# Attention: the softmax difference moved behind the next block's maxima, scores split from their maxima, two transposes later

## The chip, the cores and the metric

The kernel runs on one core of a Trainium2 chip. The metric is device time in microseconds (us) of one execution; lower is better. Five engines work from queues of their own, each strictly in the order in which its instructions stand: TensorE (PE in the rows; its weight loads are PEld), VectorE (DVE), ScalarE (ACT), GpSimd (POOL) and the queue that issues DMAs (SP).

## What is computed

One inference step of a small decoder: a convolution layer with a feed-forward layer, then a differential-attention layer with a feed-forward layer, for a prompt of 512 tokens and for 8 samples of 8 new tokens each with 512 cached positions. The change touches the attention of the prompt. Every head has two score matrices (c = 0, 1) and its weights are the difference of two softmaxes:

```python
def diff_weights(scores, q_pos, k_pos, rel_bias, lam):
    dist = q_pos[:, None] - k_pos[None, :]
    bias = jnp.transpose(rel_bias[rel_buckets(jnp.maximum(dist, 0))], (2, 0, 1)).astype(jnp.float32)
    logits = scores + bias[None, :, None]
    logits = jnp.where((dist >= 0)[None, None, None], logits, -jnp.inf)
    p = jax.nn.softmax(logits, axis=-1)
    return p[:, :, 0] - lam * p[:, :, 1]
```

`prompt_diff_attn` does this for 8 heads and 4 blocks of 128 queries; block i sees 128 (i + 1) keys. Its result times the values is normalised per head and goes through an output projection.

## The kernel before

All of it is one program for one core, written with tiles; a wrapper (line 62) keeps every engine's instructions in the order in which the Python code emits them, so nearly every row of the profile says L62 and is told apart by its tiles. The first part (convolution, feed-forward, projections to keys, queries and values) and the last part (output projection, second feed-forward) are not touched.

The attention stage is a plan of turns. `at(r, rank, f)` (line 1042) puts a function into turn r; `play` (line 1333) runs the functions of a turn by rank. Each function emits its instructions for all engines, so the ranks set the order on every engine at once. Head h takes four turns, and four more functions of older work are woven into each:

- **sample turn**, r = 4h: scores, maxima and exponent of sample h (`sample`, lines 1045 to 1154).
- **block-3 turn**, r = 4h + 1: the scores of query block 3 (512 keys), VectorE's maxima over them, ScalarE's exponentials (`prompt`, `scores`, line 1182). At its start stands `norm` of the sample (rank 0.2); behind the maxima stand the transposes of an older sample's output with ScalarE's copy of it to `xhi` (rank 2.2), and a 128x512 `xlo` of an older head (rank 2.5).
- **block-2 turn**, r = 4h + 2: the same for block 2 (384 keys); `low` of the sample, two small `xlo` (rank 0.5); `power` of the head before (rank 2.5): five VectorE operations, then GpSimd's `pow` of 128x4.
- **last-blocks turn**, r = 4h + 3: the same for blocks 1 and 0 (256 and 128 keys); values of an older sample (rank 2.47); `scale` of the head before (rank 2.3).

In `prompt` every block goes through four functions. `scores` issues six matmuls per block from `whi` and `wlo` into the two PSUM banks `bS[0]` and `bS[1]` (one for each c), and in the same function the maxima: a custom VectorE operation that adds the bias `Tb`, writes `pt` and leaves the row maximum in a small tile `sm`, followed by ScalarE's exponential. The next block's scores use the same two banks, so they wait for these maxima. `differ` (line 1205) is VectorE's: a reciprocal, a 128x1 product with lambda (`nlam`) and one pass over `pt`. `turn` (line 1218) transposes the result on TensorE (`c_rev,pt`) and copies it on ScalarE to `aT`. `values` multiplies by `vv`. Small tiles come from a pool of six buffers, `pt` from three, so a later tile can stand in the buffer of an earlier one and waits for its last reader.

```python
at(r, 2, scores)
at(r + 1, 0, differ)
at(r + 1, 5, turn)
at(r + 2, 5.1 if 3 in blocks else 3, values)
```

Of the kernel before, what the change touches and what calls it, by code (L numbers as in the profile page):

```python
# [36 lines left out]
def build(tc, A, O):  # L37
# [3 lines left out]
    with ctx:  # L41
# [38 lines left out]
        def sm(n=8):  # L80
            t = small.tile([128, 16], F32, name="sm")
            return t[:, :n]
# [529 lines left out]
        with tc.tile_pool(name="h0", bufs=1) as hp0:  # L612
# [29 lines left out]
            with tc.tile_pool(name="cv", bufs=1) as cvp:  # L642
                c = cvp.tile([128, KT, T], F32, name="c")
                smid = Stats()
                with tc.tile_pool(name="u", bufs=2) as up:
# [143 lines left out]
                    r = smid.tok_half(0)  # L789
# [18 lines left out]
                    for i, (k, hf) in enumerate(steps):  # L808
# [5 lines left out]
                        if i == 0:  # L814
                            r = smid.tok_half(1)
# [38 lines left out]
        with tc.tile_pool(name="kvq", bufs=1) as kp:  # L854
# [164 lines left out]
            with tc.tile_pool(name="att", bufs=2) as ap_:  # L1019
# [15 lines left out]
                def next_turn():  # L1035
                    turns[0] += 1
                    return bT[turns[0] % 2]
# [4 lines left out]
                def at(r, rank, f):  # L1042
                    plan.setdefault(r, []).append((rank, f))
# [134 lines left out]
                def prompt(X, blocks, r):  # L1178
                    st_ = {}
                    place = {i: (0 if x == 0 else 128 * (blocks[0] + 1)) for x, i in enumerate(blocks)}  # L1180

                    def scores():
                        pt_ = ap_.tile([128, 1024], F32, name="pt", bufs=3)
                        for i in blocks:
                            o, n = 2 * place[i], 256 * (i + 1)
                            st_[i] = (pt_[:, o:o + n].rearrange("p (c n) -> p c n", c=2), sm())
                        for i in blocks:
                            n, o = 128 * (i + 1), place[i]
                            for x, (a, b) in enumerate(((0, 0), (0, 1), (1, 0))):
                                for cc in range(2):  # L1190
                                    rows = slice(64 * cc, 64 * cc + 64)
                                    pe.matmul(bS[cc][:, o:o + n], lhsT=X.q2[a][rows, i * 128:(i + 1) * 128],
                                              rhs=X.k2[b][rows, :n], start=(x == 0), stop=(x == 2))
                        for i in blocks:
                            n, o = 128 * (i + 1), place[i]
                            t, m = st_[i]
                            for cc in range(2):
                                ve.tensor_tensor_reduce(out=t[:, cc, :], in0=bS[cc][:, o:o + n],
                                                        in1=X.Tb[:, 512 - n:512], scale=-1.0, scalar=3.0e38,
                                                        op0=ALU.add, op1=ALU.min, accum_out=m[:, cc:cc + 1])  # L1200
                                ac.activation(out=t[:, cc, :], in_=t[:, cc, :], func=AF.Exp, scale=-1.0,
                                              bias=m[:, cc:cc + 1],
                                              accum_out=(X.s0[:, i:i + 1] if cc == 0 else m[:, 2:3]))

                    def differ():
                        for i in blocks:
                            t, m = st_[i]
                            ve.reciprocal(out=m[:, 3:4], in_=m[:, 2:3])
                        for i in blocks:
                            t, m = st_[i]  # L1210
                            ve.tensor_scalar(out=m[:, 4:5], in0=X.s0[:, i:i + 1], scalar1=nlam, scalar2=m[:, 3:4],
                                             op0=ALU.mult, op1=ALU.mult)
                        for i in blocks:
                            t, m = st_[i]
                            ve.scalar_tensor_tensor(out=t[:, 0, :], in0=t[:, 1, :], scalar=m[:, 4:5],
                                                    in1=t[:, 0, :], op0=ALU.mult, op1=ALU.add)

                    def turn():
                        pT = next_turn()
                        o = 0  # L1220
                        for i in blocks:
                            for j in range(i + 1):
                                pe.transpose(out=pT[:, o + j * 128:o + (j + 1) * 128],
                                             in_=st_[i][0][:, 0, j * 128:(j + 1) * 128], identity=rev)
                            o += 128 * (i + 1)
                        aT = st_["aT"] = ap_.tile([128, 512], F32, name="aT", bufs=2)
                        ac.copy(out=aT[:, :o], in_=pT[:, :o])

                    def values():
                        o = 0  # L1230
                        for i in blocks:
                            for j in range(i + 1):
                                pe.matmul(X.po[:, i * 128:(i + 1) * 128],
                                          lhsT=st_["aT"][:, o + j * 128:o + (j + 1) * 128],
                                          rhs=vv[:, j, X.h * 128:(X.h + 1) * 128], start=(j == 0), stop=(j == i))
                            o += 128 * (i + 1)

                    at(r, 2, scores)
                    at(r + 1, 0, differ)
                    at(r + 1, 5, turn)  # L1240
                    at(r + 2, 5.1 if 3 in blocks else 3, values)

                def prompt_out(X, r):
# [52 lines left out]
                for h_ in range(H):  # L1296
                    X = Head()
                    X.last = h_ == H - 1
                    r = 4 * h_ + 1
                    sample(h_, r - 1)  # L1300
                    at(max(r - 3, 0), 6 if h_ else 0, lambda X=X, h_=h_: prepare(X, h_))
                    at(max(r - 1, 0), 0.1, lambda X=X: prepare_low(X))
                    prompt(X, (3,), r)
                    prompt(X, (2,), r + 1)
                    prompt(X, (1, 0), r + 2)
                    prompt_out(X, r + 4)
# [197 lines left out]
```

## Time and profile before

| | |
|---|---|
| median of 3 runs | 1350.44 us (1347.79 to 1351.11) |
| the profiled execution, its own time | 1349.65 us |
| its span | 1347.8 us |
| instructions | 25258 |
| TensorE matmul busy | 1329.7 us, 99% |
| TensorE weight loads busy | 1225.5 us, 91% |
| VectorE busy | 918.1 us, 68% |
| ScalarE busy | 599.1 us, 44% |
| GpSimd busy | 117.9 us, 9% |
| block-3 maxima of head 1 and of head 7, first row | at 803.21 and at 884.76 us of the span |

The profile shows one execution. Busy shares are averages over stages that have different limits, so the attention stage has to be read by itself. In the rows of the timeline the first number is the start in us from the beginning of the span, the second what the instruction (or the run of equal instructions) took; in square brackets stands the idle time of the engine before it, and what ended it. A matmul row covers several passes; its end is modelled.

### The profile page before, as it was taken

To read this page: it belongs to the slowest core of one execution; us is meant where nothing else is said; L and a number is where in the kernel's file an instruction comes from. 1 tells how busy PE (TensorE), PEld (TensorE's weight loads), DVE (VectorE), ACT (ScalarE), POOL (GpSimd) and SP (SyncE) were. 2 spreads that over 40 slices of the span, in tenths; PEclk is the share of its full clock that TensorE was granted. 3 is DMA by queue.
4 is the path that set the end of the run, shared out by engine and by line. 5 is a ranking of instruction groups with operands and counts; after the bars stand their busy time and mean duration, and the time that the engine had idled before them with its cause. 6 is when DMAs were issued, how large, how long until landed. Compare 5 with 4: busy or idle time off the path is not lost.

```text
span 1347.8 us, 25258 instructions
## 1 busy us (share of the span) xinstructions
PE 1329.7 (99%) x10320; PEld 1225.5 (91%) x10320; DVE 918.1 (68%) x1803; ACT 599.1 (44%) x1224; POOL 117.9 (9%) x112
## 2 busy tenths in 40 slices
PE   8999899999999999999999999999999999999998
PEld 7988399999999999998787766689999999999998
DVE  6999276798747757864555258876679855865862
ACT  5122273345524524544455347764434543543550
POOL 0001112000000000012222203232100000000000
PEclk9999999999999999999999999999999999999999
DMA  8765412131231231163214268964121331231121
GB/s 306 202 173 168 103 63 95 32 125 63 95 126 63 94 126 63 59 215 113 79 72 176 73 254 312 347 234 168 32 95 63 110 111 63 97 123 63 63 95 71
DMA packets 57398, 168.00 MB, mean 125 GB/s; under 512 B 5970, under 2 KB 12754, under 8 KB 57154
## 3 DMA queue, kind: packets, MB, share of 16 engines
q1 hardware_dynamic: 55552, 163.85, 34.8%
q10 hardware_dynamic: 1730, 2.54, 0.6%
q8 instruction: 81, 1.33, 0.4%
q14 instruction: 35, 0.29, 0.1%
HBM read 145.56 MB, written 10.56 MB: 116 GB/s over the span
## 4 chain that ended last, share of the span: by engine, by line
PE 82%; DVE 12%; ACT 3%; DMA 1%; SPq 1%; issue 1%; POOL 0%; DVEq 0%; ACTq 0%
PE ps L62 82%; DVE c L62 4%; DVE xlo L62 2%; DVE wlo L62 2%; DVE t L62 2%; ACT xhi L62 1%; SPq L723 1%; ACT t L62 1%; DVE u L62 1%; DMA up<-u 0%; DVE xhi L62 0%; DMA h<-in_xT 0%; ACT L62 0%; DMA u<-in_state 0%; DMA c_vec<-in_vec 0%
## 5 line engine op out<-in xcount | busy, mean ns | idle before, releaser
L62 PE MATMUL ps<-xhi,whi 128*128 128x288 f32 x1776 | 414.0, 297 | 8.8 <-ACT xhi L62 8.1
L62 PE MATMUL ps<-xhi,wlo 128*128 128x288 f32 x1648 | 394.2, 296 | 0.0
L62 PE MATMUL ps<-xlo,whi 128*128 128x288 f32 x1520 | 367.6, 297 | 0.6 <-DVE xlo L62 0.5
L62 ACT CAST whi<-raw 128x512 fp32r<-128x512 f32 (+2 forms) x425 | 242.6, 593 | 155.3 <-PE ps L62 100.2
L62 PEld LDWEIGHTS ps<-xhi,whi 128*128 128x128 f32 x1776 | 296.4, 189 | 12.7 <-ACT xhi L62 8.9
L62 DVE TENSOR_TENSOR wlo<-raw,whi 128x512 fp32r<-128x512 f32 (+2 forms) x421 | 283.1, 690 | 26.9 <-ACT whi L62 25.9
L62 PEld LDWEIGHTS ps<-xhi,wlo 128*128 128x128 f32 x1648 | 279.1, 189 | 0.0
L62 PEld LDWEIGHTS ps<-xlo,whi 128*128 128x128 f32 x1520 | 258.6, 189 | 2.1 <-DVE xlo L62 1.9
L62 PE MATMUL ps<-xhiu,whi 128*128 128x288 f32 x832 | 224.7, 295 | 0.0
L62 PE MATMUL ps<-xlou,whi 128*128 128x288 f32 x832 | 224.5, 295 | 0.0
L62 PE MATMUL ps<-xhiu,wlo 128*128 128x288 f32 x832 | 224.0, 294 | 0.0
L62 PEld LDWEIGHTS ps<-xhiu,whi 128*128 128x128 f32 x832 | 149.2, 188 | 0.2
L62 PEld LDWEIGHTS ps<-xlou,whi 128*128 128x128 f32 x832 | 149.2, 188 | 0.0
L62 PEld LDWEIGHTS ps<-xhiu,wlo 128*128 128x128 f32 x832 | 149.2, 188 | 0.0
L62 DVE TENSOR_TENSOR t<-ps,t 128x288 f32<-128x288 f32 x172 | 75.0, 451 | 56.7 <-PE ps L62 45.7
L62 DVE TENSOR_TENSOR h<-ps,h 128x288 f32<-128x288 f32 x112 | 45.9, 451 | 71.7 <-PE ps L62 71.7
L62 DVE TENSOR_TENSOR t<-t 128x576 f32<-128x576 f32 (+1 forms) x53 | 39.6, 747 | 61.6 <-ACT t L62 60.6
L62 PE MATMUL ps<-whi,xhi 128*128 128x512 f32 x192 | 76.5, 398 | 0.0
L62 PE MATMUL ps<-wlo,xhi 128*128 128x512 f32 x192 | 76.0, 396 | 0.0
L62 PE MATMUL ps<-whi,xlo 128*128 128x512 f32 x192 | 75.8, 395 | 0.0
L62 DVE TENSOR_TENSOR raw<-raw 128x512 f32<-128x512 f32 x108 | 74.1, 686 | 1.2
L62 ACT COPY t<-ps 128x288 f32<-128x288 f32 x114 | 45.3, 397 | 46.0 <-PE ps L62 45.9
(144 smaller groups left out, 1422.8 us busy)
## 6 DMA issues: line engine op xcount, KB each, us to landing
raw<-in_w_gu SPq DMA_DIRECT2D x22, 2048.0 KB, 7.7
raw<-in_w_dn SPq DMA_DIRECT2D x12, 1536.0 KB, 6.4
raw<-in_ck SPq DMA_DIRECT2D x32, 512.0 KB, 7.0
raw<-in_cv SPq DMA_DIRECT2D x32, 512.0 KB, 5.9
raw<-in_w_kvq SPq DMA_DIRECT2D x6, 2048.0 KB, 8.9
raw<-in_w SPq DMA_DIRECT2D x5, 2048.0 KB, 8.2
up<-u SPq DMA_DIRECT2D x20, 270.0 KB, 4.2
us<-u SPq DMA_DIRECT2D x32, 144.0 KB, 3.5
```

Of the source, the lines that this page charges most:

```text
L62: r = f(*a, **k)
L723: nc.sync.dma_start(out=dt_[:, j, :], in_=bass.AP(tensor=src.tensor, offset=src.offset, ap=[list(src.ap[0]), [st_, 4], [1, n]]))
```

## The change

The diff splits `scores` in two: the matmuls are at rank 1.8 of their turn and the maxima with their exponentials at rank 2. `differ` of blocks 3 and 2 goes from the start of the following turn (rank 0) to rank 2.2, right behind that turn's maxima; for blocks 1 and 0 it stays. `turn` of block 3 goes from rank 5 of the following turn to rank 1.9 of the one after, behind that turn's score matmuls. `turn` of block 2 goes from rank 5 to rank 5.2, that is behind the `values` of block 3 (5.1). Nothing is added, removed or resized, and no DMA is moved.

```diff
@@ -1191,6 +1191,8 @@
                                     rows = slice(64 * cc, 64 * cc + 64)
                                     pe.matmul(bS[cc][:, o:o + n], lhsT=X.q2[a][rows, i * 128:(i + 1) * 128],
                                               rhs=X.k2[b][rows, :n], start=(x == 0), stop=(x == 2))
+
+                    def maxima():
                         for i in blocks:
                             n, o = 128 * (i + 1), place[i]
                             t, m = st_[i]
@@ -1235,9 +1237,10 @@
-                    at(r, 2, scores)
-                    at(r + 1, 0, differ)
-                    at(r + 1, 5, turn)
+                    at(r, 1.8, scores)
+                    at(r, 2, maxima)
+                    at(r + 1, 2.2 if blocks[0] > 1 else 0, differ)
+                    at(*{3: (r + 2, 1.9), 2: (r + 1, 5.2), 1: (r + 1, 5)}[blocks[0]], turn)
                     at(r + 2, 5.1 if 3 in blocks else 3, values)
```

On VectorE, the start of a block-2 turn: `xlo 128x512` closes the block-3 turn, `xlo 128x4x8` is the sample's `low`, `ISA pt,sm<-ps,Tb 128x384` with the `ISA sm` behind it are block 2's maxima, and the last three rows are `differ` of block 3.

```order
 L62 SCALAR_TENSOR_TENSOR xlo_8461<-ps,gsub,xhi_8460 128x512
+L62 SCALAR_TENSOR_TENSOR xlo_8461<-ps,gsub,xhi_8460 128x4x8 x2
+L62 ISA pt,sm<-ps,Tb 128x384
+L62 ISA sm 128x1
+L62 ISA pt,sm<-ps,Tb 128x384
+L62 ISA sm 128x1
 L62 RECIPROCAL sm<-sm 128x1
 L62 TENSOR_SCALAR sm<-sm,nlam 128x1
 L62 SCALAR_TENSOR_TENSOR pt<-pt,sm 128x512
```

`low` and the maxima now stand ahead of the difference instead of behind it.

On VectorE, the end of a block-2 turn and the last-blocks turn of the changed program, with waits: the first row is the last of `power`, the next eight are the maxima of blocks 1 and 0, the last three `differ` of block 2. The wait on `Pool_49` is for the `pow` that GpSimd does on the result of the first row: the tile `sm_8723` stands in the buffer that `pow` reads. The program before has the same wait at the same instruction.

```order
L62 TENSOR_SCALAR sm_8695<-sm_8695 128x4 [waits DVE_49]
L62 ISA pt_8721,sm_8722<-ps_8238,Tb_8493 128x256 [waits PE_49]
L62 ISA sm_8722 128x1
L62 ISA pt_8721,sm_8722<-ps_8239,Tb_8493 128x256 [waits PE_49]
L62 ISA sm_8722 128x1
L62 ISA pt_8721,sm_8723<-ps_8238,Tb_8493 128x128 [waits Pool_49]
L62 ISA sm_8723 128x1
L62 ISA pt_8721,sm_8723<-ps_8239,Tb_8493 128x128
L62 ISA sm_8723 128x1
L62 RECIPROCAL sm_8681<-sm_8681 128x1 [waits Activation_49]
L62 TENSOR_SCALAR sm_8681<-sm_8499,nlam_92,sm_8681 128x1 [waits DVE_49]
L62 SCALAR_TENSOR_TENSOR pt_8680<-pt_8680,sm_8681 128x384 [waits DVE_49]
```

`differ` of block 2 stood between the first row and the maxima before; now the maxima follow `power` directly.

On TensorE, from the scores of block 2 to the scores of the next sample (`raw,qz`): `c_rev,pt x4` is the transposes of block 3, `c_rev,pt x3` those of block 2, `vv,aT x4` the values of block 3, `raw,aTs` and `vv,aTs` values of samples.

```order
 L62 MATMUL ps<-wlo,whi 128x384 x6
 L62 MATMUL ps<-raw,aTs 32x256 x8
-L62 MATMUL ps<-c_rev,pt 128x128 x4
 L62 MATMUL ps<-wlo,whi 128x256 x6
 L62 MATMUL ps<-wlo,whi 128x128 x6
+L62 MATMUL ps<-c_rev,pt 128x128 x4
 L62 MATMUL ps<-raw,aTs 32x256 x8
 L62 MATMUL ps<-vv,aTs 32x256 x4
+L62 MATMUL ps<-vv,aT 128x128 x4
 L62 MATMUL ps<-c_rev,pt 128x128 x3
-L62 MATMUL ps<-vv,aT 128x128 x4
 L62 MATMUL ps<-raw,qz 32x512 x8
```

The scores of blocks 1 and 0 come ahead of block 3's transposes, and block 2's transposes are now the last work ahead of the sample's scores.

## Rows read from the trace of the kernel before

**Rows 1.** Busy us, 840 to 870: PE, PEld, DVE, ACT, POOL; PE clock, DMA share, GB/s.

```profile
840.00:870.00 30.00, 30.00 (x331) 20.14 (x323) 26.76 (x106) 21.17 (x62) 9.29 (x10) 1.00 0.89 330
```

**Rows 2.** VectorE's waits, 806.07 to 887.55 us (six heads): sum, times, longest.

```profile
DVE sm L62 <- ACT t L62: 3.6, 6, 0.6
DVE sm L62 <- ACT pt L62: 2.2, 6, 0.4
```

**Rows 3.** Timeline, block-3 turn into block-2 turn of one head.

```profile
829.95 0.16 DVE L62 RECIPROCAL sm<-sm 128x1 f32<-128x1 f32 x1 [0.60 <-ACT t L62]
...
832.50 0.19 ACT L62 ACTIVATION_READ_ACCUMULATOR pt<-pt,sm 128x1 f32 x1
832.60 0.37 ACT L62 ACTIVATE xhi<-ps,gsub 128x64 fp32r<-128x64 f32 x1
832.67 0.80 PE L62 MATMUL ps<-wlo,whi 64*128 64x384 f32 x6
832.72 0.16 DVE L62 RECIPROCAL sm<-sm 128x1 f32<-128x1 f32 x1 [0.37 <-ACT pt L62]
...
833.23 0.75 DVE L62 SCALAR_TENSOR_TENSOR pt<-pt,sm 128x512 f32<-128x512 f32 x1
...
833.90 0.45 DVE L62 SCALAR_TENSOR_TENSOR xlo<-ps,gsub,xhi 128x32 fp32r<-128x32 f32 x2
834.25 0.55 DVE L62 CUSTOM_DVE_ANT_0 pt<-ps,Tb 128x384 f32<-128x384 f32 x1
834.40 0.66 PE L62 MATMUL ps<-c_rev,pt 128*128 128x128 f32 x4
...
834.99 1.26 PE L62 MATMUL ps<-wlo,whi 64*128 64x256 f32 x12
...
835.21 0.18 DVE L62 RECIPROCAL sm<-ps 128x4 f32<-128x4 f32 x1
```

**Rows 4.** Timeline, the same head: end of the block-2 turn to the next norm.

```profile
836.39 0.17 DVE L62 TENSOR_SCALAR sm<-sm 128x4 f32<-128x4 f32 x1
836.47 0.15 DVE L62 RECIPROCAL sm<-sm 128x1 f32<-128x1 f32 x1
...
836.73 1.01 POOL L62 TENSOR_TENSOR sm<-sm,mhalf 128x4 f32<-128x4 f32 x1 [7.91 <-ACT aT L62]
836.97 0.62 DVE L62 SCALAR_TENSOR_TENSOR pt<-pt,sm 128x384 f32<-128x384 f32 x1
...
837.50 0.42 DVE L62 CUSTOM_DVE_ANT_0 pt<-ps,Tb 128x256 f32<-128x256 f32 x1
...
837.75 0.55 PE L62 MATMUL ps<-c_rev,pt 128*128 128x128 f32 x3
...
838.13 1.06 PE L62 MATMUL ps<-vv,aT 128*128 128x128 f32 x8
...
838.19 0.28 DVE L62 CUSTOM_DVE_ANT_0 pt<-ps,Tb 128x128 f32<-128x128 f32 x1
...
838.61 0.39 DVE L62 TENSOR_TENSOR sm<-sm 128x4 f32<-128x4 f32 x1
...
839.11 1.92 PE L62 MATMUL ps<-raw,qz 128*32 128x512 f32 x16
...
841.47 0.68 DVE L62 CUSTOM_DVE_ANT_0 t<-ps,sbias 128x512 f32<-128x512 f32 x1
...
841.88 0.69 ACT L62 ACTIVATE xhi<-ps,gsub 128x512 fp32r<-128x512 f32 x1 [1.43 <-PE ps L62]
...
842.63 0.78 ACT L62 ACTIVATE t<-t,sm 128x576 f32<-128x576 f32 x1
...
843.54 0.17 DVE L62 RECIPROCAL sm<-sm 128x1 f32<-128x1 f32 x1 [0.60 <-ACT t L62]
```

**Rows 5.** Timeline, after the last head: VectorE waiting for GpSimd's pow.

```profile
902.46 0.17 DVE L62 TENSOR_SCALAR sm<-sm 128x4 f32<-128x4 f32 x1
...
903.76 0.16 DVE L62 TENSOR_TENSOR sm<-sm 128x4 f32<-128x4 f32 x1 [1.12 <-POOL sm L62]
```

## The prediction

> **What bounds the attention stage.** I read the busy times of the stretch first, then the waits of VectorE, then one head in the timeline.
>
> In a stretch of 30 us in the middle of the stage the matmul row is busy all of the time, the weight loads 20.14 us and VectorE 26.76 us [rows 1]; the reader should see that two engines look full. The waits decide between them: over six heads VectorE waits twice per head, always for ScalarE, 0.6 and 0.4 us [rows 2], and never for TensorE. One head takes 843.54 - 829.95 = 13.59 us from one `norm` to the next [rows 3, 4], and between those two places these two waits are the only ones of VectorE that the view lists. So the round that sets the period runs through VectorE and ScalarE: `norm`, the maxima of block 3, `differ`, the maxima of block 2, `power`, the maxima of blocks 1 and 0, `scale`, the sample's maxima, ScalarE's exponent, `norm`. What the change does to this round, it does in every head. The weight loads' 20.14 of 30 us say that TensorE still has room. (The Trainium skill, Perfetto Trace Analysis, section Identifying the Most-Contended Engine, judges TensorE's headroom by weight loads and model FLOPs and calls matmul busy time a bad measure; by that rule the trace's 20.14 us agree with VectorE as the bound. By the matmul row alone the stage would be TensorE's, and the VectorE order worth nothing: rival 3 below.)
>
> **The block-2 turn.** The wait of 0.37 us ahead of `differ` is for ScalarE's exponentials of block 3 [rows 3]. It goes, since `differ` now comes later. But the first instruction in its place is the sample's `low`, and that reads the `xhi` of 128x64 that ScalarE copies only after the same exponentials: 832.60 + 0.37 = 832.97 [rows 3]. VectorE is free at 832.72 - 0.37 = 832.35, so with the hand-over of 0.03 that its wait there shows (832.50 + 0.19 = 832.69 to 832.72) it waits to 833.00: 0.65 instead of 0.37. `low` holds it for 834.25 - 833.90 = 0.35, to 833.35. Block 2's maxima then need the scores, whose matmuls end at 832.67 + 0.80 = 833.47 [rows 3]: another 0.15, start 833.50. From there nothing is new: maxima 835.21 - 834.25 = 0.96, `differ` 833.90 - 832.72 = 1.18, `power` 836.47 - 835.21 = 1.26 [rows 3, 4]; end 836.90 instead of 836.47. **+0.43 us.**
>
> **The last-blocks turn.** After `power` the maxima of blocks 1 and 0 follow at once. Their scores come earlier than before, as their matmuls no longer stand behind block 3's transposes (0.66 us at 834.40 [rows 3]) and only wait for block 2's maxima. The fifth row of these maxima waits for GpSimd's `pow`. Before, that cost nothing: `differ` of block 2 (837.50 - 836.47 = 1.03) lay between, `pow` ended at 836.73 + 1.01 = 837.74, the row came at 838.19 [rows 4], 0.45 later. That cover is now behind it. `power`'s last row starts at 836.39 + 0.43 = 836.82; `pow` ends 837.74 - 836.39 = 1.35 after that, at 838.17; with 0.03 VectorE goes on at 838.20. The maxima of block 1 take 838.19 - 837.50 = 0.69 and leave it idle from 836.90 + 0.69 = 837.59. **+0.61 us.** How soon VectorE resumes after GpSimd is shown once elsewhere: there the wait ended 903.76 - 902.46 = 1.30 after the start of the row that fed `pow` [rows 5], so 1.30 to 1.38 bounds it, and the term is 0.53 to 0.61. I take the upper, from this very place.
>
> **TensorE behind it.** Block 3's transposes wait for `differ` (ends 834.46 + 833.98 - 832.72 = 835.72) and delay the sample values to about 836.4 instead of 836.2; that is paid for later. Block 2's transposes are now last ahead of the sample's scores. `differ` of block 2 starts at 838.20 + 0.42 (the maxima of block 0, 838.61 - 838.19) = 838.62 and ends 837.59 - 836.47 = 1.12 later, at 839.74. The hand-over to TensorE is 0.05 (834.35 to 834.40 [rows 3]) to 0.16 (837.59 to 837.75 [rows 4]); with 0.10 the transposes start at 839.84, need 838.13 - 837.75 = 0.38, and about 0.1 goes to the change of shape; the sample's scores start at 840.32 instead of 839.11: +1.21. What follows them on TensorE is the transpose whose result ScalarE copies at 841.88 for 0.69, and in ScalarE's queue the sample's exponent stands right behind that copy, at 842.63 [rows 4]. So `norm` comes about **1.19** later. VectorE by itself would be later by 0.43 + 0.61 and, as blocks 1 and 0 are no longer differenced right behind their exponentials, earlier by some 0.06: 0.98. The longer path counts: 13.59 + 1.19 = 14.8 us per head.
>
> **The sum.** Heads 1 to 7 have all of this: 7 x 1.19 = 8.3. Head 0 has no `power`, hence no `pow` to wait for, and overlaps the projections; it is worth between nothing and 1.2; I take 1.19 - 0.61 = 0.6. After the last head TensorE runs the first matmuls of the output projection without a break, so nothing is won back there. The moved score matmuls and transposes are the same instructions; no DMA moves, and page loads that are issued later have no fewer turns to land. The profiled execution took 1349.65 us, so 1349.65 + 8.9 = **1358.5 us**. It lies 0.8 below the median shown, 1350.44; from the median the sum would be 1359.3, inside the range. A measurement of this kernel can tell some 0.3% (4 us) from no change.
>
> **Rivals.**
>
> 1. *GpSimd is not waited for* (its spans in the profile are rough, and the buffer could come free sooner). Then 0.61 falls away on both paths: 1.19 - 0.61 = 0.6 per head, 8 x 0.6 = 4.8, 1354.4 us. For it: only the program's order shows that wait, no row does. Against it: rows 5 show VectorE held for just such a `pow`.
> 2. *No net change.* The 0.60 wait of `norm` could take up the shift, if ScalarE's exponent did not move with VectorE; then little is left, 1350 us. Against it: the exponent starts only when the sample's maxima are done (842.63 [rows 4]), so that wait moves along with them.
> 3. *Faster: TensorE is the bound.* Its matmul row has no idle time [rows 1]. If it set the period, VectorE's delays would be slack, and what counts is that the scores of blocks 1 and 0 start as soon as the banks are free rather than behind block 3's transposes: at most 834.99 - 834.40 = 0.59 per head, 8 x 0.59 = 4.7, 1344.9 us. It decides if VectorE's two waits per head were for work that TensorE delivered late. Against it: they are for ScalarE, whose input came from VectorE [rows 2, 3].
> 4. *Slower still*, over 1362 us: if the later copies on ScalarE or the page loads queue up behind one another; at 0.4 more per head this begins. Nothing in the rows points there.
>
> **How the numbers follow.** My forecast gets 0.65, rival 1 0.15, rival 2 0.10, rival 3 0.06, rival 4 0.04. The forecast's own spread is 0.98 x 7 (VectorE alone, nothing for head 0) = 6.9 to 1.3 x 8 = 10.4, that is 1356.5 to 1360. The range goes down to take in rival 1 with a margin, and up by the distance of the median: 1352 to 1362; rivals 2 to 4, 0.20 together, lie outside. Faster by over 0.3%: 0.06. Within 0.3% (1346.4 to 1354.5): rival 2 and half of rival 1, since its 1354.4 lies on that edge: 0.17. Slower: 0.77.
>
> **What would show it.** The period between the first maxima rows of block 3 should go from 13.59 to 14.6 to 14.9 us. VectorE's waits should show per head: `xlo` of 128x32 behind ScalarE's `xhi`, about 0.65; `sm` or `pt` of 128x128 behind GpSimd's `sm`, about 0.6; the 0.37 ahead of the reciprocal of block 3 gone. TensorE's load row should show waits of some 0.4 and 0.9 us ahead of the two sets of transposes. I am wrong if the period stays below 13.9 us or VectorE shows no wait for GpSimd; if the wait for `xhi` stays under 0.4 us, the first term is wrong; if VectorE's waits are as forecast but the period grows by 1.0 only, the path through block 2's transposes is.

## The result, and the profile after

| | before | changed |
|---|---|---|
| median, on the same chip | 1349.68 us (1347.79 to 1351.11, 4 runs) | 1360.88 us (1360.49 to 1362.88, 4 runs) |
| profiled execution, its span | 1349.65 us, 1347.8 us | 1362.88 us, 1361.1 us |
| period, block-3 maxima of head 1 to head 7, a sixth of it | 13.59 us | 15.46 us |

The changed kernel is slower: its time is 1.0092 times that of before, with an interval of 1.0079 to 1.0105. The 1350.44 us shown ahead of the prediction times 1.0092 is 1362.9 us, just above the range of 1352 to 1362 around the forecast of 1358.5; the median of the changed kernel itself, 1360.88, lies inside it. The sign and the two waits were as forecast. The size was not: the period grew by 1.87 us per head instead of 1.19.

The busy times of the same 30 us as in [rows 1], by engine in the order PE, PEld, DVE, ACT, POOL:

```profile
840.00:870.00 30.00, 28.12 (x284) 18.09 (x284) 25.36 (x93) 19.57 (x56) 8.99 (x8) 1.00 0.81 298
```

All engines do less in this stretch, since a head takes longer. TensorE's matmul row now has idle time, and the clock is granted in full as before. VectorE's waits over 806 to 900 us (sum, times, longest), against [rows 2]:

```profile
DVE xlo L62 <- ACT xhi L62: 5.2, 7, 1.3
DVE sm L62 <- ACT t L62: 3.6, 6, 0.6
DVE pt L62 <- POOL sm L62: 3.2, 6, 0.5
```

The 0.4 ahead of block 3's difference is gone. `low` waits for `xhi` in its place (the 1.3 is head 1's; in the others it is 0.64 to 0.66), and the maxima of block 0 wait for GpSimd's `pow` in every head. Both were forecast. `norm`'s 0.60 stayed. These waits do not explain the whole growth, and the rest can only be seen in what single instructions take. The timeline of one head shows it, from `norm` (849.46) to the next `norm` (864.93), 15.47 us later; the first rows answer to [rows 3], those from 856.32 on to [rows 4]:

```profile
849.46 0.16 DVE L62 RECIPROCAL sm<-sm 128x1 f32<-128x1 f32 x1 [0.60 <-ACT t L62]
...
852.12 0.36 ACT L62 ACTIVATE xhi<-ps,gsub 128x64 fp32r<-128x64 f32 x1
...
852.51 0.46 DVE L62 SCALAR_TENSOR_TENSOR xlo<-ps,gsub,xhi 128x32 fp32r<-128x32 f32 x2 [0.64 <-ACT xhi L62]
...
856.32 0.17 DVE L62 TENSOR_SCALAR sm<-sm 128x4 f32<-128x4 f32 x1
...
856.66 1.01 POOL L62 TENSOR_TENSOR sm<-sm,mhalf 128x4 f32<-128x4 f32 x1 [8.34 <-ACT aT L62]
...
857.09 0.08 DVE L62 DVE_READ_ACCUMULATOR2_ANT sm<- 128x1 f32 x1
...
857.64 1.27 POOL L62 TENSOR_TENSOR whi<-xlo,whi 128x512 fp32r<-128x512 f32 x1
857.71 0.29 DVE L62 CUSTOM_DVE_ANT_0 pt<-ps,Tb 128x128 f32<-128x128 f32 x1 [0.54 <-POOL sm L62]
...
858.64 0.69 DVE L62 SCALAR_TENSOR_TENSOR pt<-pt,sm 128x384 f32<-128x384 f32 x1
...
858.87 1.59 POOL L62 TENSOR_TENSOR wlo<-xhi,wlo 128x512 fp32r<-128x512 f32 x1
859.25 1.23 DVE L62 TENSOR_TENSOR sm<-sm 128x4 f32<-128x4 f32 x1
859.39 0.55 PE L62 MATMUL ps<-c_rev,pt 128*128 128x128 f32 x3 [0.79 <-DVE pt L62]
859.86 1.92 PE L62 MATMUL ps<-raw,qz 128*32 128x512 f32 x16
...
860.52 0.69 DVE L62 TENSOR_TENSOR t<-ps,sm 128x512 f32<-128x512 f32 x1
...
862.63 0.69 ACT L62 ACTIVATE xhi<-ps,gsub 128x512 fp32r<-128x512 f32 x1 [2.19 <-PE ps L62]
...
862.87 0.68 DVE L62 CUSTOM_DVE_ANT_0 t<-ps,sbias 128x512 f32<-128x512 f32 x1
...
864.03 0.78 ACT L62 ACTIVATE t<-t,sm 128x576 f32<-128x576 f32 x1 [0.71 <-DVE sm L62]
...
864.93 0.16 DVE L62 RECIPROCAL sm<-sm 128x1 f32<-128x1 f32 x1 [0.60 <-ACT t L62]
```

A walk along VectorE, each place counted from its own `norm`, gives the account:

| stretch on VectorE | before | after | growth |
|---|---|---|---|
| `norm` to `power`'s last row | 6.44 | 6.86 | +0.42 |
| wait for `pow` (857.09 to 857.71) | 0 | 0.62 | +0.62 |
| rest of the way to `scale`'s 128x4 product | 2.22 | 2.31 | +0.09 |
| the product, to the next row | 0.43 | 1.27 | +0.84 |
| to the sample's maxima | 2.43 | 2.35 | -0.08 |
| to the next `norm` | 2.07 | 2.06 | -0.01 |
| sum | 13.59 | 15.47 | +1.88 |

The line that no step of the prediction has is the fourth. `scale`'s product multiplies 128x4 numbers, took 0.39 us before [rows 4], and now takes 1.23. It shows no wait: the time is inside the instruction. It ends at 860.48, and the second of GpSimd's two 128x512 casts ends at 858.87 + 1.59 = 860.46.

### The profile page after: what moved, and what is told of

It reads as the page before. It is cut to its first block, busy times and chain, and to the rows that moved or that the text cites. A ratio compares the mean times of both kernels' runs of the same rounds, so it can differ in the third digit from the quotient of the medians.

```text
span 1361.1 us, 25258 instructions
## 1 busy us (share of the span) xinstructions
PE 1335.1 (98%) x10320; PEld 1226.9 (90%) x10320; DVE 927.4 (68%) x1803; ACT 601.6 (44%) x1224; POOL 120.3 (9%) x112
## 4 chain that ended last, share of the span: by engine, by line
PE 79%; DVE 15%; ACT 3%; DMA 1%; issue 1%; POOL 1%; SPq 0%; DVEq 0%; ACTq 0%; POOLq 0%
PE ps L62 79%; DVE c L62 5%; DVE xlo L62 2%; DVE wlo L62 2%; DVE t L62 2%; DVE pt L62 2%; ACT xhi L62 1%; ACT t L62 1%; DVE sm L62 1%; POOL sm L62 1%; DVE u L62 1%; DVE xhi L62 0%; DMA up<-u 0%; SPq L723 0%; DMA h<-in_xT 0%
```

## The theory and its rivals

**Theory.** A VectorE operation that has two inputs in SBUF is not finished while one of GpSimd's two 128x512 casts runs. The casts (`prepare_low`) subtract the high parts of the next head's queries and keys and stand behind `pow` in GpSimd's queue. Before, the first fell on the maxima of blocks 1 and 0 and the second on a 128x512 product and some 128x1 columns; the maxima and the 128x512 product read PSUM and at most one tile of SBUF. The 128x4 product was held for the end of the first cast only (838.61 + 0.39 = 839.00 [rows 4]). In the changed program `differ` of block 2 (its pass over `pt`: two SBUF inputs) and the product come later, and fall on the first cast's end and on the whole of the second. The casts of the kernel before, with two 128x4 products of `power` ahead of them:

```profile
835.99 0.36 DVE L62 TENSOR_TENSOR sm<-sm 128x4 f32<-128x4 f32 x2
...
837.71 1.27 POOL L62 TENSOR_TENSOR whi<-xlo,whi 128x512 fp32r<-128x512 f32 x1
...
838.95 1.27 POOL L62 TENSOR_TENSOR wlo<-xhi,wlo 128x512 fp32r<-128x512 f32 x1
```

**Rivals.** That the product is late for a reason of its own (its producers, TensorE's reads); that the wait for `pow` is what costs; that TensorE's path through block 2's transposes, on which the prediction built its 1.19, sets the period. Ten kernels tell them apart. The period is the distance of the first rows of block-3 maxima of consecutive heads. Where no interval stands beside a time, it is that of a single execution, so the period carries the comparison there. The diffs show the main lines of each edit, against the changed kernel, with `...` where lines are left out.

## Experiments: the two halves of the change

**Block 3 alone.** `differ` and `turn` of block 3 moved as in the change; block 2 as before.

```diff
-                    at(r + 1, 2.2 if blocks[0] > 1 else 0, differ)
-                    at(*{3: (r + 2, 1.9), 2: (r + 1, 5.2), 1: (r + 1, 5)}[blocks[0]], turn)
+                    at(r + 1, 2.2 if blocks[0] > 2 else 0, differ)
+                    at(*{3: (r + 2, 1.9), 2: (r + 1, 5), 1: (r + 1, 5)}[blocks[0]], turn)
```

> Only block 3's difference and transposes moved; block 2's difference and transposes stay where they were before. Theory: only the first term of the prediction is left, the wait for the sample's copy and for the scores of block 2, 0.42 per head: period 14.0 us; no wait for GpSimd, and the 128x4 product takes 0.4 as before. Rival (the terms come from the score matmuls issued apart, or from block 3's transposes standing later on TensorE): a period of 14.5 or more here.

Measured: 1352.83 us, period 14.00. The growth is 0.41, the first term of the prediction (0.43). The product is as it was before, held to the end of the first cast (867.39 + 1.28 = 868.67):

```profile
867.39 1.28 POOL L62 TENSOR_TENSOR whi<-xlo,whi 128x512 fp32r<-128x512 f32 x1
...
868.29 0.39 DVE L62 TENSOR_TENSOR sm<-sm 128x4 f32<-128x4 f32 x1
```

**Block 2 alone.** The other half.

```diff
-                    at(r + 1, 2.2 if blocks[0] > 1 else 0, differ)
-                    at(*{3: (r + 2, 1.9), 2: (r + 1, 5.2), 1: (r + 1, 5)}[blocks[0]], turn)
+                    at(r + 1, 2.2 if blocks[0] == 2 else 0, differ)
+                    at(*{3: (r + 1, 5), 2: (r + 1, 5.2), 1: (r + 1, 5)}[blocks[0]], turn)
```

> Only block 2's difference and transposes moved; block 3's stay where they were before. Theory: wait for GpSimd 0.54, the 128x4 product held to the end of GpSimd's second cast (0.84 more than before), little else: period 14.9 to 15.0 us, and no wait for the sample's copy. Rival (the hold needs the shift of 0.42 by block 3 as well): product at 0.4, period 14.1 to 14.4, set by the wait for GpSimd and by block 2's transposes.

Measured: 1359.42 us, period 15.06, growth 1.47, with the wait of 0.54 for GpSimd and a product of 1.23. The two halves add up: 0.41 + 1.47 = 1.88. So the unforecast part belongs to block 2.

```profile
855.43 0.29 DVE L62 CUSTOM_DVE_ANT_0 pt<-ps,Tb 128x128 f32<-128x128 f32 x1 [0.54 <-POOL sm L62]
...
856.98 1.23 DVE L62 TENSOR_TENSOR sm<-sm 128x4 f32<-128x4 f32 x1
```

## Experiments: the wait, the product, the casts

**Nine small buffers** instead of six, so that the maxima of block 0 no longer stand in the buffer that `pow` reads.

```diff
-        small = pool("small", 6)
+        small = pool("small", 9)
```

> The changed kernel, with nine buffers for the small tiles instead of six, so that the maxima of block 0 no longer share a buffer with the input of GpSimd's `pow`. Theory (hold by the casts): the wait for GpSimd (0.54) goes, the 128x4 product then arrives 0.54 earlier, inside the first cast instead of the second, is let go between the two as in the kernel before, and takes 0.2 to 0.4 instead of 1.23: period 14.0 to 14.3 us, so much more than the wait itself is won. Rival (the two costs are separate and add): only 0.54 is won, period 14.9, the product still takes 1.2.

Measured: 1362.78 us, period 15.5. The wait is gone and nothing was won; both expectations missed. The timeline says where the time went:

```profile
856.42 1.27 POOL L62 TENSOR_TENSOR whi<-xlo,whi 128x512 fp32r<-128x512 f32 x1
...
856.79 1.32 DVE L62 SCALAR_TENSOR_TENSOR pt<-pt,sm 128x384 f32<-128x384 f32 x1
857.64 1.59 POOL L62 TENSOR_TENSOR wlo<-xhi,wlo 128x512 fp32r<-128x512 f32 x1
858.03 1.23 DVE L62 TENSOR_TENSOR sm<-sm 128x4 f32<-128x4 f32 x1
```

Since VectorE no longer waits, its pass over `pt` starts earlier, now beside the first cast, and takes 1.32 us instead of 0.62. The product behind it again ends with the second cast (857.64 + 1.59 = 859.23; 858.03 + 1.23 = 859.26). In this order VectorE comes through behind the casts whether it waits for `pow` or not. The pass is the second operation with two SBUF inputs that is held.

**The product on GpSimd**, right behind `pow`.

```diff
+                        po_.tensor_tensor(out=sc[:, 4:8], in0=sc[:, :4], in1=r0[:, :4], op=ALU.mult)
...
-                        ve.tensor_tensor(out=sc[:, 4:8], in0=sc[:, :4], in1=r0[:, :4], op=ALU.mult)
```

> The changed kernel, with the 128x4 product of `scale` moved from VectorE to GpSimd, behind `pow` (same result). In the changed kernel this product takes 1.23 us on VectorE and ends with GpSimd's second cast. Theory (VectorE's operations with two inputs in SBUF are held while GpSimd runs): VectorE loses the 1.23, and the path over block 2's transposes takes over, period 14.6 to 14.9 us instead of 15.47. Rival (the time is a delay that some other VectorE operation would meet in its place, such as the power of GpSimd arriving late): the next VectorE operation takes over the wait, period 15.3 to 15.5.

Measured: 1358.33 us, period 15.00, between the two expectations. The product takes GpSimd 0.20 us and delays the casts by that; the first now lies further over the pass over `pt`:

```profile
869.65 1.27 POOL L62 TENSOR_TENSOR whi<-xlo,whi 128x512 fp32r<-128x512 f32 x1
...
870.38 0.95 DVE L62 SCALAR_TENSOR_TENSOR pt<-pt,sm 128x384 f32<-128x384 f32 x1
870.88 1.59 POOL L62 TENSOR_TENSOR wlo<-xhi,wlo 128x512 fp32r<-128x512 f32 x1
```

The pass ends 0.41 behind the cast's end (870.92), 0.33 longer than undisturbed. In this run `norm` waits 0.78 instead of 0.60, and the sample's maxima wait 0.18 for TensorE: with the product gone, the longer path is the prediction's own, through block 2's transposes. Its 14.78, and 0.33 for the pass ahead of the transposes, make 15.1; from the 14.66 that the run without casts shows (below) it is 14.99.

**No casts.** Heads 1 to 7 use the low parts of head 0, which leaves GpSimd's casts out there.

```diff
+                    if first_low:
+                        X.q2[1], X.k2[1] = first_low
+                        return
+                    first_low.extend((X.q2[1], X.k2[1]))
```

> The changed kernel without GpSimd's two 128x512 casts of the low parts in heads 1 to 7; these heads use the low parts of head 0, so this work is left out and seven heads compute with other numbers. Theory (a VectorE operation with two SBUF inputs isn't finished while GpSimd runs one of these casts): the 128x4 product of scale takes 0.15 to 0.2 us instead of 1.23, the 128x384 pass of differ 0.62 instead of 0.69, and the wait for pow stays at 0.5 us; VectorE's path loses 1.1 us, TensorE's path of the prediction (13.59 + 1.19) may take over: period 14.3 to 14.8 us, 1352 to 1356 us in all. Rival (the product is held by something else, its producers or TensorE's reads): it still takes 1.2 us and the period stays at 15.3 to 15.5, 1360 to 1362 us.

Measured: 1358.03 us, period 14.66: 1.07 per head over before, inside the theory's span. The total that I had put beside it was too low for such a period: 7 x 1.07 and 0.6 for head 0 are 8.1 us. The two operations are back at their own length, the wait for `pow` is unchanged at 0.53, and `norm` now waits 0.78:

```profile
832.23 0.16 DVE L62 RECIPROCAL sm<-sm 128x1 f32<-128x1 f32 x1 [0.78 <-ACT t L62]
...
841.49 0.62 DVE L62 SCALAR_TENSOR_TENSOR pt<-pt,sm 128x384 f32<-128x384 f32 x1
...
842.02 0.15 DVE L62 TENSOR_TENSOR sm<-sm 128x4 f32<-128x4 f32 x1
...
842.64 1.92 PE L62 MATMUL ps<-raw,qz 128*32 128x512 f32 x16
```

The product takes 0.15 us when no cast runs and 1.23 when one does: the casts hold it, and the rival that it is late for a reason of its own is out. What is left is the prediction's path through block 2's transposes: the sample's scores start 842.64 - 832.23 = 10.41 after `norm` instead of 839.11 - 829.95 = 9.16 [rows 3, 4], and the period is 14.66 where the prediction had 14.78.

**No casts, and nine small buffers.**

> As the run without casts (heads 1 to 7 use the low parts of head 0: work left out), and the small tiles have nine buffers instead of six, so that nothing waits for pow. Theory: neither the wait of 0.54 us nor the holds are left; VectorE keeps only the first term, 0.42 per head, and TensorE's path shrinks with it: period 14.0 to 14.3 us, 1350 to 1353 us in all. Rival (the wait for pow was not worth anything, as in the run with nine buffers and casts): period as without casts, 14.3 to 14.8.

Measured: 1353.78 us, period 14.03 (mean of six). The wait for `pow` is worth something once the casts are out of the way: 0.63 per head. What is left, 0.44, has the size of the first term, but that does not show that it is the first term: `norm` waits 0.78 to 0.94 here, as it does where the exponent stands behind ScalarE's copy to `xhi`, hence behind TensorE.

```profile
829.49 0.16 DVE L62 RECIPROCAL sm<-sm 128x1 f32<-128x1 f32 x1 [0.78 <-ACT t L62]
```

## Experiments: the casts elsewhere, and the order on TensorE

**Casts one head ahead**, behind the sample's `power`; the complete program, nine small buffers. (The tiles that they read are prepared earlier too; the load of `Tb` stays where it was.)

```diff
-                    at(max(r - 1, 0), 0.1, lambda X=X: prepare_low(X))
+                    at(*((r - 5, 2.1) if h_ > 1 else (max(r - 1, 0), 0.1)), lambda X=X: prepare_low(X))
```

> The changed kernel, complete: the casts of each head's low parts are prepared one head earlier and stand behind the sample turn's power, where VectorE has no operation with two SBUF inputs for some us, and the small tiles have nine buffers. Theory: both the wait for pow and the holds go, period 14.0 to 14.3 us, 1350 to 1353 us in all; what is left of the change's cost is its first term. Rival (the hold comes with the order of the change and not with the place of the casts): period 15.0 or more, 1358 us or more.

Measured: 1356.05 us, period 14.37 (five of six distances; the last is 13.73): better than the change by 1.1 per head, but short of the expectation. A third operation is held there, one that I had not counted, `norm`'s 128x88 product:

```profile
830.32 1.28 POOL L62 TENSOR_TENSOR wlo<-xhi,wlo 128x512 fp32r<-128x512 f32 x1
...
830.71 0.95 DVE L62 TENSOR_SCALAR cs<-c_comb,sm,cvec 128x88 f32<-128x88 f32 x1
```

It takes 0.95 us instead of 0.33, and ends (831.66) just after the cast (831.60). It has one tile as input and two columns as scalars, so "two SBUF inputs" is not the whole rule. Of the 0.62 that it loses, about 0.3 is absorbed at block 2's maxima, which otherwise wait for their scores (0.19 in the next run). The last distance, 0.64 shorter, ends at head 7, beside whose `norm` no cast stands: there the 128x88 product takes 0.33 again, in the same execution.

**Casts behind block 3's maxima**, one head ahead, tied to them by a small GpSimd product that reads them.

```diff
+                    if X.h > 1:
+                        m = last_m[-1]
+                        po_.tensor_tensor(out=gate[:, 0:2], in0=m[:, 0:2],
+                                          in1=m[:, 0:2], op=ALU.mult)
...
-                    at(*((r - 5, 2.1) if h_ > 1 else (max(r - 1, 0), 0.1)), lambda X=X: prepare_low(X))
+                    at(*((r - 4, 2.1) if h_ > 1 else (max(r - 1, 0), 0.1)), lambda X=X: prepare_low(X))
```

> The changed kernel, complete, with nine small buffers and the casts of the next head placed in the block-3 turn: a 128x2 product on GpSimd that reads block 3's maxima stands ahead of them, so that they run from there on, some 4 us in which VectorE has no 128x88 product and no pass with two SBUF inputs. Theory (the hold moved from scale's product to norm's 128x88 product when the casts stood behind the sample's power): cs<-c_comb takes 0.33 us again instead of 0.95, scale's product 0.15, no wait for GpSimd; period 14.0 to 14.3 us as in the run that left the casts out, 1351 to 1354 us in all. Rival (casts hold any VectorE pass that reads SBUF, wherever they stand): xlo 128x512 and block 2's maxima, which now run beside the casts, take longer than 0.74 and 0.55, period 14.6 or more, 1356 us or more.

Measured: 1356.60 us (1354.65 to 1356.81), ratio 1.0050 [1.0034, 1.0065], period 14.02. The period is in the theory's span, the same as with the casts left out:

```profile
833.08 0.16 DVE L62 RECIPROCAL sm<-sm 128x1 f32<-128x1 f32 x1 [0.78 <-ACT t L62]
833.28 0.33 DVE L62 TENSOR_SCALAR cs<-c_comb,sm,cvec 128x88 f32<-128x88 f32 x1
...
835.12 1.28 POOL L62 TENSOR_TENSOR whi<-xlo,whi 128x512 fp32r<-128x512 f32 x1
...
836.35 1.29 POOL L62 TENSOR_TENSOR wlo<-xhi,wlo 128x512 fp32r<-128x512 f32 x1
836.72 0.56 DVE L62 CUSTOM_DVE_ANT_0 pt<-ps,Tb 128x384 f32<-128x384 f32 x1 [0.19 <-PE ps L62]
...
842.25 0.16 DVE L62 TENSOR_TENSOR sm<-sm 128x4 f32<-128x4 f32 x1
...
842.87 1.92 PE L62 MATMUL ps<-raw,qz 128*32 128x512 f32 x16
```

The casts run beside block 2's maxima, which read `ps` and one tile of SBUF, and neither loses anything (0.56, and 1.28 and 1.29). The holds and the wait for `pow` together are worth 1.44 per head, 15.46 to 14.02. What sets the remaining 0.43 is not VectorE alone: the sample's scores start 842.87 - 833.08 = 9.79 after `norm` instead of 9.16, and `norm` waits 0.78, nearly as in the run with TensorE's order alone (below: 9.81, and a period of 14.06). The total is some 3 us more than this period gives (7 x 0.43 + 0.6); in the profiled execution 1.7 of it lie ahead of head 0's first maxima, at 790.43 instead of 788.72. Why was not settled.

**The order on TensorE alone**: scores apart from maxima and the two `turn`s where the change has them, `differ` where it was.

```diff
-                    at(r + 1, 2.2 if blocks[0] > 1 else 0, differ)
+                    at(r + 1, 0, differ)
```

> The kernel before with the part of the change that is TensorE's alone: scores apart from their maxima, block 3's transposes behind the scores of blocks 1 and 0, block 2's behind the values of block 3; differ stays where it was. Theory (what the change costs comes from differ's place on VectorE): period 13.5 to 13.6 us, ratio 0.999 to 1.001. Rival 1 (block 2's transposes as the last work ahead of the sample's scores delay these by themselves): period 13.8 or more, 1351.5 us or more. Rival 2 (the earlier scores of blocks 1 and 0 are worth their 0.59 per head): period 13.0, 1345 to 1347 us.

Measured: 1353.34 us (1352.54 to 1355.34), ratio 1.0035 [1.0023, 1.0047], period 14.06 (one of the six distances is 15.43; there TensorE stood idle for 1.3 us ahead of the sample's scores, for a cause that is not settled, and it is left out). My theory missed: TensorE's order by itself costs 0.47 per head. That is the first rival's period, but not its mechanism.

```profile
834.40 1.38 PE L62 MATMUL ps<-wlo,whi 64*128 64x256 f32 x12 [0.32 <-DVE sm L62]
...
836.30 1.07 PE L62 MATMUL ps<-raw,aTs 128*32 128x256 f32 x16
...
839.28 1.92 PE L62 MATMUL ps<-raw,qz 128*32 128x512 f32 x16
...
841.27 0.69 DVE L62 CUSTOM_DVE_ANT_0 t<-ps,sbias 128x512 f32<-128x512 f32 x1 [0.18 <-PE ps L62]
...
843.53 0.17 DVE L62 RECIPROCAL sm<-sm 128x1 f32<-128x1 f32 x1 [0.78 <-ACT t L62]
```

With block 3's transposes out of the way, TensorE's next work is the scores of blocks 1 and 0, and these wait 0.32 us for block 2's maxima. The transposes filled that gap before. The sample values behind them start 836.30 - 829.47 = 6.83 after `norm`; before it was 836.18 - 829.95 = 6.23:

```profile
836.18 1.07 PE L62 MATMUL ps<-raw,aTs 128*32 128x256 f32 x16
```

The sample's scores start 839.28 - 829.47 = 9.81 after `norm` instead of 9.16, and `norm` waits 0.18 longer. So 0.60 of the 0.65 is lost ahead of the sample values, and the last place of block 2's transposes adds only 0.05 as long as `differ` stays early.

**Before, with the casts one head ahead, nine small buffers and the product on GpSimd**, to see whether the hold that the kernel before already has (0.39 instead of 0.15) can be won back.

> The kernel before (none of the change) with the casts moved one head ahead as in the run casts-ahead, nine small buffers, and the 128x4 product of scale moved to GpSimd behind pow. Theory: VectorE loses the product (0.39) and what else the casts held, about 0.43 per head: period 13.1 to 13.3 us instead of 13.59, 3 us less in all, 1346 to 1348 us, ratio 0.9975 to 0.9985. Rival (TensorE or ScalarE sets the period of the kernel before): period stays at 13.5 to 13.6, ratio 0.9995 to 1.0005.

Measured: 1354.76 us (1352.59 to 1357.62), ratio 1.0042 [1.0027, 1.0058], period 14.48 (the last distance is 13.66): slower, which neither expectation had.

```profile
844.94 1.27 POOL L62 TENSOR_TENSOR wlo<-xhi,wlo 128x512 fp32r<-128x512 f32 x1
...
845.12 1.15 DVE L62 TENSOR_SCALAR cs<-c_comb,sm,cvec 128x88 f32<-128x88 f32 x1
...
855.66 0.16 DVE L62 RECIPROCAL sm<-sm 128x1 f32<-128x1 f32 x1 [0.49 <-ACT pt L62]
```

The 128x88 product is held (1.15 instead of 0.33: 0.82), and the 0.39 of the removed product came back as a wait of 0.49 for ScalarE's exponentials of blocks 1 and 0. The last distance ends at head 7, beside whose `norm` no cast stands: it is 0.82 shorter, 13.66, and still not below 13.59. So without the hold the period stays near the old one, as the rival has it: a wait for ScalarE takes the place of the product. No version that beats both kernels came out of these runs.

## Why the prediction was right and wrong

- **The block-2 turn, +0.43: right.** The walk gives +0.42, and block 3 alone 0.41. VectorE waits 0.64 for `xhi` (forecast 0.65), and the wait for block 3's exponentials is gone.
- **The last-blocks turn, +0.61: right as a wait.** From the end of block 1's maxima to block 0's first row it is 0.62. But the wait's worth hung on what stands behind it: removed by itself it won nothing, since the held pass took its place; with the casts left out it is worth 0.63.
- **The path through block 2's transposes: right in its numbers.** The sample's scores start 859.86 - 849.46 = 10.40 after `norm`, 1.24 later than before (forecast 1.21), and without the casts, where this path sets the period, that is 14.66 (forecast 14.78). It missed one thing: block 3's transposes had filled a gap, and moving them away costs TensorE 0.47 per head even where `differ` stays early.
- **"VectorE by itself would be later by 0.43 + 0.61 and ... earlier by some 0.06: 0.98. The longer path counts": this step failed.** The three terms are right (0.42, 0.62, -0.08). Missing is a fourth, put at nothing without a reason, of 0.93 per head: the product 0.84 and the pass over `pt` with what surrounds it 0.09, both held by GpSimd's casts. VectorE's path is 1.88; TensorE's is at most 1.24, and 1.07 in the period of the run without casts. So the longer path is the other one. In the changed kernel the exponent waits 0.71 for VectorE's maxima, long after `xhi` (862.63 + 0.69 = 863.32).
- **The sum.** With 1.88 in place of 1.19 it is 1349.65 + 7 x 1.88 + 0.6 = 1363.4; the profiled execution took 1362.88. It was the longest of four; the others took 1360.49 to 1361.12, and no trace shows where they are 2 us shorter. Head 0 grew by 0.68 (788.36 to 803.53, against 788.72 to 803.21), forecast 0.6. That this is right is partly luck: with block 3's half alone head 0 grows by 0.80 (788.34 to 803.63), with block 2's alone by 0.03 (788.36 to 802.88), so block 2's transposes, on which the forecast built its 1.19, have no part in it.
- **The rivals.** GpSimd is waited for, the 0.60 moved along, and TensorE's order gained nothing. Rival 4, slower still by 0.4 or more per head, is what came (0.68), but neither by ScalarE's copies, behind which the exponent no longer stands, nor by a wait of VectorE for page loads.

A row gave the hint. The product's 0.39 [rows 4] is over twice the 0.18 that each of `power`'s two 128x4 products takes (0.36 for both, 855.93 after and 835.99 before), and it ends at 839.00, with the first cast's end at 837.71 + 1.27 = 838.98. I took 0.39 as its length and moved it, without asking what would run beside it in the new place.

## What to carry to other kernels

An instruction that takes longer than its twins elsewhere in the same trace may be held, even where the profile shows no wait ahead of it; look for what ends when it ends. Before moving work on VectorE, lay GpSimd's instructions over the new place as well: a hand-placed order like this one may owe its speed to which operations run beside GpSimd's casts. A cost that comes out in the size expected can still come from another path: look again at what the last instruction of the round waits for. And where removing a wait wins nothing, compare what the instructions behind it take before and after.

## What the runs showed of the hardware

**Some VectorE operations and GpSimd's casts hold each other up.** A 128x4 product with both inputs in SBUF takes 0.15 us alone and 1.23 beside a 128x512 cast of GpSimd; a 128x384 pass with two inputs 0.62 alone and up to 1.32; a 128x88 product with one tile and two scalar columns 0.33 alone, 0.95 and 1.15. Each held operation is over 0.0 to 0.4 us after the cast's end. It goes the other way too: a cast that is issued while VectorE's pass runs takes 1.59 us instead of 1.27. Maxima that read PSUM and one tile of SBUF keep their 0.56 beside a cast. Not all of GpSimd's work holds: in the kernel before, the 128x384 pass with its two inputs takes its 0.62 at 836.97, inside the 1.01 that the 128x4 `pow` takes from 836.73 on [rows 4]; spans on GpSimd are rough, so this is less firm than the rest.

The Trainium skill, SBUF — State Buffer, section Who interferes with whom, has this as a rule: the pair of ports that GpSimd and VectorE share goes to whichever operation starts first, for the whole instruction, and the other is blocked; a VectorE operation takes part if it has two SBUF inputs and GpSimd reads SBUF, or if it runs in a mode that uses both ports for one tensor, which `tensor_scalar` can. The casts agree in both orders and for both kinds (1.23 and 1.59; 0.95 for the `tensor_scalar` of 128x88). The 128x4 `pow` does not: the pass that starts during its span is not blocked. That the 128x88 product runs in such a mode is taken from the Trainium skill; the runs show only that it is held.

**TensorE's order mattered although its weight loads had room.** The load row was at 20.14 of 30 us before [rows 1], and the order alone cost 0.47 per head: what counted was the place of one gap of 0.32 us and what stood in the queue behind it, not the share.
